# Three token mixers in another order: forgetting, then with sinks, then compressed

## The chip, the cores and the metric

The kernel runs on one core of a Trainium2 chip. Its engines are named as in the profile: PE (TensorE matmul), PEld (its weight loads), DVE (VectorE), ACT (ScalarE), POOL (GpSimd), SP (SyncE, which issues most DMAs). The metric is the device time of one execution in microseconds.

## What is computed

One layer of a decoder trunk on 1024 tokens of 1024 channels, in float32. One projection of the normalised input feeds three causal token mixers and the gates that merge them:

```
h = rms_norm(x, norm_mix);  cols = split_columns(h @ w_in)
o_a = nsa_mixer(...)   # A (number 0): compressed blocks, 8 selected blocks of 64 keys,
                       #   a window of 256, joined by sigmoid gates per head
o_b = swa_mixer(...)   # B (number 1): window of 128, with a learned sink per head
o_c = fox_mixer(...)   # C (number 2): dense causal, a cumulative log forget gate on the logits
branches = stack([o_a, o_b, o_c]);  proj = einsum('btnm,nmd->btnd', branches, w_branch)
gates = sigmoid(cols['merge']).reshape(b, t, 3, 1024)
x = x + (gates * proj).sum(axis=2) @ w_out
x = x + conv_ffn(rms_norm(x, norm_ffn), w_gate, w_up, conv_w, conv_b, w_down)
```

Each mixer has 8 heads of 64. The mixers don't need each other: any order of the three gives the same sum.

## The kernel before

Every product is made of three matmuls on halves that are rounded to a shorter format (high x high, high x low, low x high: lines 258 to 260). So each float32 operand is split first: ACT makes the high half (a CAST), DVE the low half (a subtraction). Weights are split in `wload` (raw `wraw`, halves `whi` and `wlo`, lines 234 and 235, two rows of 128 at a time).

The part that matters here is the woven one, from about 165 us on. The order on PE is written out there by a planner (class `Line`, `drive`), which merges three streams with its own clock and its own guesses of durations; the other engines are ordered by the scheduler around it.

- The first stream, `attend`, runs the mixers one after the other: `fox` (C), `mixer_a` (A), `mixer_b` (B). A unit of attention is two matmuls into an S bank (line 685, and 687 or 689), a minimum on DVE (704 or 700), an exp on ACT (713, `p<-S`), for B one more exp for the sink (753, `es`), sums and a reciprocal on DVE (754, 756), and a scaling of `p` on POOL (762). After each mixer its number is put as a mark into the queue of jobs.
- The second stream turns the scaled `p` (transposes into a T bank, line 797), splits the result on ACT and DVE (`pTh` 804, `pTl` 805) and multiplies it with V into the one O bank (820, 821). `out_bank` empties O (885 on ACT, 886 on DVE) and stores it to `s_o`.
- The third stream, `fill`, is dense work for the gaps: chunks of the projection by token (`tok_chunk`; 256 or 280 columns into a D bank, ACT copies at 426, squares and powers on POOL at 432 and 437, DVE at 435 and 440), then the 12 chunks of merge gates (`gate_chunks`; 512 columns, DVE 493, ACT 494), then the merges of two mixers. `merge(n)` waits for the mark of mixer n, loads its eight tiles of `s_o` into the `xl` buffers (line 1363), splits them (1364 on ACT, 1365 on DVE), and multiplies with `w_branch`.

The last gate chunk is made in another order (`lo_first`): it reads the low halves `xl` of the input first (line 512) so that `xl` comes free for the tiles of `s_o`, and then the high halves (484, 485). So the splits of the first merge fall beside the second half of this chunk.

There are 3 S banks, 2 T, 1 O and 2 D. What the streams leave of the fill when attention has ended is made densely; then `merge_last` does the third mixer and the rest of the program follows.

Of the kernel before, what the change touches and what calls it, by code (L numbers as in the profile page):

```python
# [167 lines left out]
class Builder:  # L168
# [291 lines left out]
    def gate_chunks(self, wp, sp, rbc):  # L460

        nc, a = self.nc, self.a
        for cc in (8, 9, 10, 11, 0, 1, 2, 3, 4, 5, 6, 7):
            n, r = divmod(cc * 256, D)
            w = self.wload(wp, a["w_in"], MERGE + cc * 256, 256, KD)
            for b in range(2):
                bs = slice(b * P, (b + 1) * P)
                for h in range(2):
                    hs = slice(h * 512, (h + 1) * 512)
                    if cc != 7 or b == 0:  # L470
                        yield self.d_free
                        p = self.dps()
                        yield from self.mm3_steps(p, [((w[k][0][:, bs], w[k][1][:, bs]),
                                                       (self.xh[k][:, hs], self.xl[k][:, hs])) for k in range(KD)],
                                                  b == 1 and h == 1)
                    else:
                        if h == 0:
                            ps = yield from self.lo_first(w, bs)
                        else:
                            yield lambda: 0.0  # L480
                        p = ps[h]
                        for k in range(KD):
                            yield lambda: 0.0
                            nc.tensor.matmul(p, w[k][0][:, bs], self.xh[k][:, hs], start=False, stop=False)
                            nc.tensor.matmul(p, w[k][1][:, bs], self.xh[k][:, hs], start=False, stop=(k == KD - 1))
                            self.line.pe(0.427)
                            if h == 1 and k % 2 == 1:
                                self.s_w.put(self.line.now)
                    t = self.line.on("V", self.line.now, 0.6)
                    self.s_d.put(t)  # L490
                    t = self.line.on("A", t, 0.52)
                    g = self.t(sp, [P, 512], F32, "stage", 3)
                    nc.vector.tensor_tensor(out=g, in0=p, in1=rbc[:, hs], op=ALU.mult)
                    nc.scalar.activation(g, g, AF.Tanh, scale=0.5)
                    out = self.s_gate[n, r + b * P:r + (b + 1) * P, hs]
                    if self.woven:
                        self.line.later(t + STORE, nc.sync.dma_start, out, g, tag="stage")
                    else:
                        nc.sync.dma_start(out, g)
# [1306 lines left out]
def run(gen):  # L1806
    for _ in gen:
        pass


def build(tc, a):
    with ExitStack() as ctx:
        b = Builder(tc, a)
        b.setup(ctx)
        pool = tc.tile_pool
        xp = b.xp = ctx.enter_context(pool(name="xp", bufs=1))
        wctx = ctx.enter_context(ExitStack())
        tp = wctx.enter_context(pool(name="tp", bufs=1))
        b.zero = b.t(tp, [P, 1], F32, "zero")
        tc.nc.vector.memset(b.zero, 0.0)  # L1820
        b.kc2 = b.t(tp, [P, P], F32, "kc2", 1)
        b.vc = [[b.t(tp, [P, P], F32R, f"vc{g}{j}", 1) for j in range(2)] for g in range(2)]
        wp = wctx.enter_context(pool(name="wp1", bufs=1))
        macc = [None] * KD
        b.mh, b.ml = {}, {}
        dense = ["D", "S", "S", "D", "S", "T", "T"]
        with pool(name="sp1", bufs=1) as sp:
            rbc = b.t(sp, [P, T], F32, "rbc", 1)
            tcm = b.t(sp, [P, NH, 128], F32, "tcm", 1)
            b.dcyc = ["D", "S", "S", "D", "S"]  # L1830
            with pool(name="s0", bufs=1) as s0:
                b.first(xp, s0, wp, sp)
            with pool(name="ctp", bufs=1) as ctp, pool(name="s1", bufs=1) as s0, pool(name="wpc", bufs=1) as wpc:
                wps = [wp, wpc]
                b.small = (wpc,)
                b.bias_rows(s0)
                b.cmp_table(tcm, s0)
                wins = [b.windows(ctp, which) for which in range(2)]
                run(b.tok_chunk(wps, sp, "cv1"))
                b.forget(s0)  # L1840
                b.compress(ctp, wps, 0, *wins[0])
                run(b.tok_chunk(wps, sp, "cq0"))
                b.compress(ctp, wps, 1, *wins[1])
                run(b.tok_chunk(wps, sp, "cv0"))
                for h in range(2):
                    b.bcast_cols(s0, b.rstd[:, h * 4:(h + 1) * 4], rbc[:, h * 512:(h + 1) * 512])
            with pool(name="ap1", bufs=1) as ap_, tc.manual_schedule(engines={mybir.EngineType.PE}):
                b.woven = True

                def attend():  # L1850
                    for n, mixer in ((2, b.fox(ap_)), (0, b.mixer_a(ap_, tcm)), (1, b.mixer_b(ap_))):
                        yield from mixer
                        b.jobs.append({"mark": n})
                    b.s_over = True

                def fill():
                    for n in ("ck1", "cq1", "ksvs", "kwvw", "aq0", "aq1", "bkv", "bq0", "bq1"):
                        yield from b.tok_chunk([wp], sp, n)
                    yield from b.gate_chunks([wp], sp, rbc)
                    for n in (2, 0):  # L1860
                        yield lambda: 0.0 if n in b.marks else NEVER
                        yield from b.merge(n, n == 2, macc, None, [wp], sp)

                b.dcyc = dense
                b.line.drive(attend(), b.t_stream(ap_), fill())
        b.dcyc = dense
        wctx.close()
        with pool(name="rp", bufs=1) as rp, pool(name="wq", bufs=1) as wq:
            b.wq = wq
            with pool(name="sp3", bufs=1) as sp:  # L1870
                b.out_proj(macc, b.merge_last(1, macc, rp, wq, sp), rp, wq, sp)
                last = b.gate_up(sp)
                with tc.manual_schedule(engines={mybir.EngineType.SP}):
                    b.down(last, rp)
# [50 lines left out]
```

## Time and profile before

| | us |
|---|---|
| median of three runs | 1880.89 (1880.38 to 1882.27) |
| the profiled execution | 1881.61 |
| its span, first to last instruction | 1879.8 |
| PE busy | 1842.3 (98%) |
| DVE busy | 1349.6 (72%) |
| ACT busy | 926.3 (49%) |
| POOL busy | 406.7 (22%) |

By the page's chain of the work that ended last, 90% of the span lies on PE. In time the woven part goes: C until about 460 us, A until about 917 us, B from 940 to 1046 us. Under C run the chunks by token; they end at about 523 us, in A. The gate chunks run from 515 to 978 us. The merge of C begins with its loads at 953 us, that of A at 1054 us; from 1064 us on `merge_last` makes that of B. An idle stretch of PE is read from the windows as length less busy time.

### The profile page before, as it was taken

What the parts mean: (1) busy time and instruction counts of PE and PEld (TensorE: products, weight loads), DVE (VectorE), ACT (ScalarE), POOL (GpSimd) and SP (SyncE); (2) the same over time, 40 slices, a digit from 0 to 9 for tenths busy, and PEclk for the clock granted to TensorE, in tenths of its full rate; (3) what the DMA queues carried; (4) which work ended last, traced back from release to release, by engine and by line L of the source; (5) the groups of instructions that cost most, each with busy time, mean ns of one, the idle gap of its engine ahead of it and who ended that gap; (6) DMA issues with size and microseconds to landing.
All of it is one profiled execution on the core that took longest, in us unless ns stands there. A gap on an engine that the chain in (4) does not pass through costs nothing.

```text
span 1879.8 us, 30674 instructions
## 1 busy us (share of the span) xinstructions
PE 1842.3 (98%) x10663; PEld 1619.8 (86%) x10663; DVE 1349.6 (72%) x2825; ACT 926.3 (49%) x1987; POOL 406.7 (22%) x586
## 2 busy tenths in 40 slices
PE   8999999999999999999989999999999999999999
PEld 8999999999988888888878888888888888878887
DVE  7664767776875666757688766669887778786865
ACT  4443566565544555546587523435443334344443
POOL 2223655565521423213232230000000000000000
PEclk9999999999999999999999999999999999999999
DMA  6345322233221132121343755534534434367433
GB/s 210 108 147 133 86 79 75 78 88 90 72 79 54 51 89 79 57 65 57 110 143 105 219 160 179 158 111 157 165 126 144 159 123 135 131 241 238 138 99 124
DMA packets 201471, 228.38 MB, mean 121 GB/s; under 512 B 43633, under 2 KB 149121, under 8 KB 201316
## 3 DMA queue, kind: packets, MB, share of 16 engines
q1 hardware_dynamic: 201252, 226.29, 39.0%
q8 instruction: 84, 1.38, 0.3%
q14 instruction: 71, 0.58, 0.1%
q0 software_dynamic: 64, 0.13, 0.0%
HBM read 162.12 MB, written 64.25 MB: 120 GB/s over the span
## 4 chain that ended last, share of the span: by engine, by line
PE 90%; DVE 5%; DMA 2%; ACT 2%; issue 1%; POOL 1%; SPq 0%; DVEq 0%; ACTq 0%; POOLq 0%
PE D L259 9%; PE D L258 9%; PE D L260 9%; PE T L797 5%; PE S L1574 3%; PE S L1572 3%; PE S L1573 3%; PE O L821 3%; PE O L820 2%; PE S L685 2%; PE T L1574 2%; PE T L1573 2%; PE T L1572 2%; PE D L1572 2%; PE D L1574 2%; PE D L1573 2%
## 5 line engine op out<-in xcount | busy, mean ns | idle before, releaser
L713 ACT ACTIVATE p<-S,mf 128x512 f32<-128x512 f32 (+3 forms) x320 | 174.4, 549 | 103.5 <-DVE mf L704 95.1
L805 DVE TENSOR_TENSOR pTl<-T,pTh 128x512 fp32r<-128x512 f32 (+2 forms) x248 | 150.9, 616 | 80.5 <-ACT pTh L804 78.8
L258 PE MATMUL D<-whi,xh 128*128 128x256 f32 (+2 forms) x680 | 199.0, 293 | 1.9 <-ACT whi L234 1.8
L1544 ACT CAST qhi<-qS 128x512 fp32r<-128x512 f32 x157 | 97.2, 622 | 205.4 <-PE O L1789 54.8
L259 PE MATMUL D<-wlo,xh 128*128 128x256 f32 (+2 forms) x680 | 192.6, 283 | 2.3 <-DVE wlo L235 2.3
L260 PE MATMUL D<-whi,xl 128*128 128x256 f32 (+2 forms) x680 | 192.1, 282 | 0.0
L804 ACT CAST pTh<-T 128x512 fp32r<-128x512 f32 (+2 forms) x248 | 128.3, 532 | 119.6 <-PE T L797 108.0
L259 PE MATMUL D<-xl,whi 128*128 128x512 f32 x448 | 176.6, 394 | 0.0
L762 POOL TENSOR_SCALAR p<-p,den,gates 128x384 f32<-128x384 f32 (+3 forms) x160 | 108.9, 694 | 270.5 <-DVE den L756 168.5
L258 PE MATMUL D<-xh,whi 128*128 128x512 f32 x368 | 152.2, 414 | 0.0
L1545 DVE TENSOR_TENSOR qlo<-qS,qhi 128x512 fp32r<-128x512 f32 x157 | 106.7, 687 | 56.0 <-ACT qhi L1544 55.2
L260 PE MATMUL D<-xh,wlo 128*128 128x512 f32 x368 | 145.0, 394 | 0.0
L797 PE MATMUL T<-c,p 128*128 128x128 f32 x864 | 129.7, 273 | 7.0 <-POOL p L762 4.1
L258 PEld LDWEIGHTS D<-whi,xh 128*128 128x128 f32 x680 | 128.6, 189 | 4.0 <-ACT whi L234 2.5
L259 PEld LDWEIGHTS D<-wlo,xh 128*128 128x128 f32 x680 | 128.8, 189 | 3.8 <-DVE wlo L235 2.9
L260 PEld LDWEIGHTS D<-whi,xl 128*128 128x128 f32 x680 | 128.6, 189 | 0.0
L235 DVE TENSOR_TENSOR wlo<-wraw,whi 128x512 fp32r<-128x512 f32 (+2 forms) x136 | 102.2, 760 | 31.5 <-ACT whi L234 25.5
L820 PE MATMUL O<-pTh,VV 128*128 128x256 f32 x448 | 119.4, 290 | 2.0 <-DVE osum L886 1.9
L821 PE MATMUL O<-pTl,VV 128*128 128x256 f32 x448 | 116.6, 284 | 2.4 <-DVE pTl L805 2.4
L762 POOL TENSOR_SCALAR p<-p,den 128x256 f32<-128x256 f32 (+3 forms) x160 | 90.5, 582 | 125.7 <-DVE den L756 47.9
L685 PE MATMUL S<-U,X 128*128 128x256 f32 (+2 forms) x320 | 107.8, 341 | 4.5 <-ACT p L713 4.3
L797 PEld LDWEIGHTS T<-c,p 128*128 128x128 f32 x864 | 100.9, 140 | 12.7 <-POOL p L762 7.9
(443 smaller groups left out, 5244.9 us busy)
## 6 DMA issues: line engine op xcount, KB each, us to landing
wraw<-w_in SPq DMA_DIRECT2D x96, 256.0 KB
s_gate<-stage SPq DMA_DIRECT2D x48, 256.0 KB
qraw<-w_up SPq DMA_DIRECT2D x24, 512.0 KB
qraw<-w_gate SPq DMA_DIRECT2D x22, 512.0 KB
xh<-w_down SPq DMA_DIRECT2D x22, 512.0 KB
s_sums<-xh SPq DMA_DIRECT2D x44, 256.0 KB
qS<-s_sums SPq DMA_DIRECT2D x44, 256.0 KB
s_act<-gc SPq DMA_DIRECT2D x20, 512.0 KB
```

Source lines behind the costliest of these rows:

```text
L258: nc.tensor.matmul(out, lh, rh, start=(k == 0), stop=False)
L259: nc.tensor.matmul(out, lh, rl, start=False, stop=False)
L260: nc.tensor.matmul(out, ll, rh, start=False, stop=(k == n - 1))
L685: nc.tensor.matmul(p, z["x"][:, z["qs"]], u[:, ks], start=True, stop=False)
L713: nc.scalar.activation(pt, z["tiles"][n][:, :w], AF.Exp, bias=z["m"], scale=-1.0, accum_out=den[:, n, q:q + 1])
L762: nc.gpsimd.tensor_scalar(pt, pt, d0[:, q:q + 1], 1.0 if gate is None else gate, op0=ALU.mult, op1=ALU.mult)
L797: nc.tensor.transpose(p[:, c0:c0 + P], z["t"][:, k:k + P], self.ident)
L805: nc.vector.tensor_tensor(out=pl[:, lo:hi], in0=p[:, lo:hi], in1=ph[:, lo:hi].bitcast(F32), op=ALU.subtract)
L820: nc.tensor.matmul(ow, vv[:, kj, :], parts["h"][:, cs], start=(b_first and s == 0), stop=False)
L821: nc.tensor.matmul(ow, vv[:, kj, :], parts["l"][:, cs], start=False, stop=(b_last and s == len(bank) - 1))
L1572: nc.tensor.matmul(p, lh[:, kk, :], rh, start=(first and kk == 0), stop=False, skip_group_check=True)
L1573: nc.tensor.matmul(p, lh[:, kk, :], rl, start=False, stop=False, skip_group_check=True)
```

## The change

The mixers run in the order C, B, A. The chunks by token follow: those of B before those of A. The gate chunks of B are made ahead of those of A, so that the chunk split in two halves is the last of A's (3 instead of 7). The two merges in the woven part are C's and B's, and `merge_last` takes A's.

```diff
-        for cc in (8, 9, 10, 11, 0, 1, 2, 3, 4, 5, 6, 7):
+        for cc in (8, 9, 10, 11, 4, 5, 6, 7, 0, 1, 2, 3):
...
-                    if cc != 7 or b == 0:
+                    if cc != 3 or b == 0:
...
-                    for n, mixer in ((2, b.fox(ap_)), (0, b.mixer_a(ap_, tcm)), (1, b.mixer_b(ap_))):
+                    for n, mixer in ((2, b.fox(ap_)), (1, b.mixer_b(ap_)), (0, b.mixer_a(ap_, tcm))):
...
-                    for n in ("ck1", "cq1", "ksvs", "kwvw", "aq0", "aq1", "bkv", "bq0", "bq1"):
+                    for n in ("ck1", "cq1", "bkv", "bq0", "bq1", "ksvs", "kwvw", "aq0", "aq1"):
...
-                    for n in (2, 0):
+                    for n in (2, 1):
...
-                b.out_proj(macc, b.merge_last(1, macc, rp, wq, sp), rp, wq, sp)
+                b.out_proj(macc, b.merge_last(0, macc, rp, wq, sp), rp, wq, sp)
```

What this does to the order is seen best at the crossing from the gates to the first merge. First ACT, before, where the eight splits of `s_o` tiles (L1364) begin; `p` with a 256-column S bank and `es` are B's:

```order
L804 CAST pTh_12364<-T_12359 128x512
L1364 CAST xl_2788_12726<-xl_2788_12726 128x512
L885 COPY osum_12383<-O_12332 64x512
L713 ACTIVATE p_12377,den_12355<-S_12373,mf_12354 128x256
L753 ACTIVATE es_12396<-mf_12354,sinks_71 128x1
L1364 CAST xl_2789_12730<-xl_2789_12730 128x512
L1364 CAST xl_2790_12734<-xl_2790_12734 128x512
L640 ACTIVATE X_12408<-T_12403,gain_65 64x512
L1364 CAST xl_2791_12738<-xl_2791_12738 128x512
L713 ACTIVATE p_12394,den_12355<-S_12390,mf_12354 128x256
L753 ACTIVATE es_12396<-mf_12354,sinks_71 128x1
```

The same place of ACT after; `p` of 384 columns is the window branch of A:

```order
L713 ACTIVATE p_12628,den_12618<-S_12622,mf_12617 128x384
L1364 CAST xl_2860_12957<-xl_2860_12957 128x512
L1364 CAST xl_2861_12961<-xl_2861_12961 128x512
L713 ACTIVATE p_12657,den_12618<-S_12651,mf_12617 128x384
L1364 CAST xl_2862_12965<-xl_2862_12965 128x512
L804 CAST pTh_12687<-T_12684 128x256
L713 ACTIVATE p_12674,den_12663<-S_12668,mf_12662 128x384
L1364 CAST xl_2863_12969<-xl_2863_12969 128x512
L1364 CAST xl_2864_12973<-xl_2864_12973 128x512
```

The splits stand among A's exps instead of B's, and the exps of sinks are gone from between them. On PE, before, the second half of the split gate chunk (L484, L485) is laid between B's logits (L685 and L687, 256 columns):

```order
L484 MATMUL D_12322<-xh_41_122,whi_12117 128x512
L485 MATMUL D_12322<-xh_41_122,wlo_12118 128x512
L685 MATMUL S_12475<-U_11944,X_12254 128x256
L687 MATMUL S_12475<-V_11945,X_12254 128x256
L484 MATMUL D_12322<-xh_42_123,whi_12123 128x512
L485 MATMUL D_12322<-xh_42_123,wlo_12124 128x512
L484 MATMUL D_12322<-xh_43_124,whi_12123 128x512
L485 MATMUL D_12322<-xh_43_124,wlo_12124 128x512
```

The same place of PE after, in A, whose logits of selected blocks (L689) are 384 and 512 columns wide:

```order
L484 MATMUL D_12602<-xh_42_123,whi_12440 128x512
L485 MATMUL D_12602<-xh_42_123,wlo_12441 128x512
L685 MATMUL S_12760<-U_11037,X_12019 128x384
L689 MATMUL S_12760<-V_11038,Y_12022 128x384
L685 MATMUL S_12770<-U_11037,X_12024 128x512
L689 MATMUL S_12770<-V_11038,Y_12027 128x512
L820 MATMUL O_12451<-pTh_12731,VV_11241 128x256
L821 MATMUL O_12451<-pTl_12732,VV_11241 128x256
```

The chunk's second half has moved from B to A. B itself stands after the change on PE beside chunks by token (L258 to L260 with 256 columns) at its start:

```order
L632 MATMUL T_6725<-c_6_69,qt_6450 128x128 x4
L685 MATMUL S_6741<-U_6161,X_6444 128x256
L687 MATMUL S_6741<-V_6162,X_6444 128x256
L820 MATMUL O_6747<-pTh_6613,VV_6254 128x256
L821 MATMUL O_6747<-pTl_6614,VV_6254 128x256
```

and a little further on, past two more logits, the fill beside it:

```order
L258 MATMUL D_6724<-whi_6702,xh_38_119 128x256
L259 MATMUL D_6724<-wlo_6703,xh_38_119 128x256
L260 MATMUL D_6724<-whi_6702,xl_46_127 128x256
L258 MATMUL D_6724<-whi_6702,xh_39_120 128x256
L259 MATMUL D_6724<-wlo_6703,xh_39_120 128x256
```

Before, the fill beside B was the end of the gate chunks and merge C.

## Rows read from the trace of the kernel before

**Rows 1.** Busy time in stretches: start:end, length, then each engine, clock, DMA.

```profile
core 0: us, PE busy (x) PEld busy (x) DVE busy (x) ACT busy (x) POOL busy (x), PEclk, DMA share, GB/s
165.00:262.00 97.00, 91.15 (x727) 89.13 (x726) 67.88 (x162) 56.08 (x136) 53.85 (x80) 0.98 0.39 104
262.00:460.00 198.00, 193.83 (x1560) 189.62 (x1559) 142.08 (x341) 120.89 (x292) 113.44 (x189) 1.00 0.31 85
460.00:940.00 480.00, 475.81 (x2870) 420.78 (x2869) 325.42 (x900) 259.15 (x628) 143.92 (x204) 1.00 0.25 72
940.00:1000.00 60.00, 52.89 (x319) 45.09 (x318) 51.48 (x159) 48.86 (x154) 17.81 (x36) 1.00 0.43 125
1000.00:1110.00 110.00, 108.83 (x570) 91.80 (x569) 81.23 (x180) 57.91 (x155) 37.26 (x46) 1.00 0.58 180
```

**Rows 2.** Waits of PE, total, times, longest: 262 to 460, 460 to 940.

```profile
PE D L258 <- ACT whi L234: 1.4, 1, 1.4
PE O L820 <- DVE osum L886: 1.3, 1, 1.3
...
PE T L797 <- POOL p L762: 1.7, 1, 1.7
```

**Rows 3.** PE in order of time: start, length, line, tiles; 512 and 256 columns.

```profile
600.12 0.40 PE L259 MATMUL D<-xl,whi 128*128 128x512 f32 x1
600.36 0.39 PE L260 MATMUL D<-xh,wlo 128*128 128x512 f32 x1
...
437.14 0.28 PE L259 MATMUL D<-wlo,xh 128*128 128x256 f32 x1
437.25 0.28 PE L260 MATMUL D<-whi,xl 128*128 128x256 f32 x1
```

**Rows 4.** Busy time in stretches: all of B, and two parts of it.

```profile
940.00:1046.00 106.00, 98.11 (x602) 85.16 (x601) 92.55 (x284) 86.23 (x272) 31.21 (x64) 1.00 0.41 120
955.00:985.00 30.00, 24.06 (x151) 20.28 (x150) 27.95 (x82) 28.04 (x85) 9.01 (x17) 1.00 0.59 176
985.00:1046.00 61.00, 60.22 (x374) 53.16 (x373) 54.19 (x165) 47.95 (x151) 18.19 (x38) 1.00 0.36 103
```

**Rows 5.** Groups by line in 940 to 1046 us: busy, mean ns, idle before.

```profile
L1387 DVE SCALAR_TENSOR_TENSOR xh<-stage,D 128x512 f32<-128x512 f32 x12 | 8.1, 678 | 1.1 <-PE D L260 1.1
L235 DVE TENSOR_TENSOR wlo<-wraw,whi 128x512 fp32r<-128x512 f32 x10 | 6.9, 695 | 0.7 <-ACT whi L234 0.7
L1365 DVE TENSOR_TENSOR xl<-xl 128x512 fp32r<-128x512 f32 x8 | 5.3, 685 | 0.7 <-ACT xl L1364 0.6
L493 DVE TENSOR_TENSOR stage<-D,rbc 128x512 f32<-128x512 f32 x4 | 2.7, 684 | 1.4 <-PE D L260 1.4
...
L753 ACT ACTIVATE es<-mf,sinks 128x1 f32<-128x1 f32 x64 | 18.5, 289 | 0.0
L234 ACT CAST whi<-wraw 128x512 fp32r<-128x512 f32 x10 | 6.0, 621 | 0.0
L1364 ACT CAST xl<-xl 128x512 fp32r<-128x512 f32 x8 | 4.7, 614 | 1.2 <-DMA xl<-s_o 1.2
L494 ACT ACTIVATE stage<-stage 128x512 f32<-128x512 f32 x4 | 2.5, 631 | 2.9 <-DVE stage L493 2.9
```

**Rows 6.** In order of time: ACT at the crossing, and a wait of PE.

```profile
955.57 0.62 ACT L1364 CAST xl<-xl 128x512 fp32r<-128x512 f32 x1 [1.23 <-DMA xl<-s_o]
...
968.40 0.39 PE L685 MATMUL S<-U,X 128*128 128x256 f32 x1 [1.40 <-ACT p L713]
```

**Rows 7.** Groups by line in 262 to 460 us, under chunks by token.

```profile
L426 ACT ACTIVATE stage<-D,rstd 128x256 f32<-128x256 f32 x38 | 16.4, 476 | 10.1 <-PE D L260 8.7 <-POOL Y L648 1.0
L235 DVE TENSOR_TENSOR wlo<-wraw,whi 128x512 fp32r<-128x512 f32 x16 | 13.7, 870 | 1.9 <-ACT whi L234 1.9
L440 DVE TENSOR_TENSOR stage<-stage,rr 128x256 f32<-128x256 f32 x18 | 7.9, 482 | 3.3 <-POOL rr L437 3.3
L435 DVE TENSOR_REDUCE rr<-sqh 128x8 f32<-128x512 f32 x10 | 6.7, 672 | 2.5 <-POOL sqh L432 2.5
```

## The prediction

> **What bounds the kernel now.** I first cut the part that the change can reach, 165 to 1110 us, into stretches [rows 1]. The reader is to see that TensorE is busy nearly throughout and that its idle time sits in places: 5.85 us of 97 before 262 us, 4.17 of 198 to 460, 4.19 of 480 to 940, 7.11 of 60 from 940 to 1000, 1.17 of 110 after. That is 22.5 us in all. After 1110 us the program is dense matmul work that the edit doesn't touch. So TensorE is the bound, its work is the same in both kernels (same matmuls, same shapes), and only these bubbles can change: the forecast is about where the new order opens and closes waits. Who ends the waits says that they are of several kinds [rows 2]: weights not yet split, the one O bank not yet emptied, a probability tile not yet scaled on POOL, an S bank not yet read by ACT.
>
> The busy figure hides some of the loss. A 512-column matmul is shown as 0.39 to 0.40 us long but the next one starts 0.23 us later; a 256-column one shows 0.28 and the next starts 0.11 to 0.12 later [rows 3]. So each wait costs about 0.16 us more than the idle time shown. The Trainium skill (Perfetto Trace Analysis, Identifying the Most-Contended Engine) says the same: matmul busy time is no good measure, since matmuls are pipelined. By its view a gain of eight removed waits would be 8 x 0.16 = 1.3 us larger than my sum of idle times; I leave that out of the sum.
>
> The worst place is 955 to 985 us: TensorE does 24.06 us of work in 30, while DVE and ACT are busy 27.95 and 28.04 [rows 4]. Two things meet there. The mixer with sinks (B) is heavy on ACT and DVE for little matmul work: every 256-column exp is followed by a 0.29 us exp of the sink [rows 5]. And the fill crosses from the gates to the merge of the forgetting mixer, which puts eight splits of s_o tiles on ACT (0.61 us each) and on DVE (0.69 us each), of which the first waits 1.23 us at the head of ACT for its DMA, with an osum copy and exps behind it in the order [rows 5, 6]. TensorE then stands for S banks, 1.40 us at 968.4 [rows 6]. Right after, from 985 to 1046, the same mixer under merge matmuls loses only 0.78 us of 61, with DVE at 54.19 and ACT at 47.95 [rows 4]. So it is the crossing inside B that costs, not B.
>
> **The change part by part.** *Up to the fourth token chunk* (about 273 us) TensorE's rows are the same in both programs: the third chunk is bkv for ksvs, of the same shapes. The 5.85 us before 262 us stay. 0.
>
> *The rest of the forgetting mixer (262 to 460 us, 4.17 us idle).* The chunks under it are bkv, bq0, bq1 and then ksvs, kwvw, instead of the A chunks first. The chunks' work is equal in sum; what moves is how they fall against the mixer. The waits here are accidents of spacing: 1.4 us for weights, 1.3 for the O bank [rows 2]. Summing the starts of rows 3 along the order, the shortest time after which TensorE comes back to the O bank is 1.2 us before and 2.8 us after; to a weight buffer 3.8 and 4.5 us. Bounds: 2 us lost (new accidents half as large again as the old) to 4.2 us gained. I take half, -2.0.
>
> *B earlier, under tokens and gates.* From B's first logits to its last, the order before holds 210 fill matmuls of 512 columns (0.23 each: 48 us) beside B's own 42 us; after, 297 of 256 columns (0.118) and 135 of 512, 66 us, beside 44. So B is spread over 110 us of matmul work instead of 90. Its own demand: in 940 to 1046 us DVE is busy 92.55 and ACT 86.23 [rows 4]; less the merge, gate, split and weight rows there (8.1 + 6.9 + 5.3 + 2.7 on DVE, 6.0 + 4.7 + 2.5 on ACT) [rows 5] that leaves 69.5 and 73.0. The fill under it after is 6.2 token banks, 5.6 gate blocks and the weight pairs of both: a token bank is two ACT copies of 0.476 us and 0.672 + 2 x 0.482 on DVE, a weight pair 0.62 on ACT and up to 0.87 on DVE [rows 7], a gate block 0.63 and 0.68 [rows 5]. Sum: 17 us on ACT, 23 on DVE. So ACT 90 and DVE 93 of 110: 82 and 84%. The nearest row is 985 to 1046 (ACT 79, DVE 89%, 0.78 lost in 61): 110 x 0.78 / 60.2 = 1.4 us lost. The upper bound is the rate of 955 to 985, if the token chunks' POOL work holds B's probabilities back; the lower is 0.
>
> *The crossing, now under A.* The eight splits stay, and fall between A's units. From the first to the last matmul of the split gate chunk the order holds 23.3 us of TensorE work after, 19.5 before. A's demand by 460 to 940 us [rows 1] is 325.42 / 475.81 = 0.68 us of DVE and 0.54 of ACT for one of TensorE: 15.9 and 12.7 us here, with the splits 21.4 and 17.6, or 92 and 76%. Before, DVE and ACT did 28 us against 24 of TensorE. So ACT, which held the S banks, gets room, and DVE is just under the matmuls. Bounds 0 and 5.9 us (the crossing as it was); I take 1.5, nearer to the row of 985 to 1046.
>
> Both together: B and its crossing lost 106 - 98.11 = 7.89 us [rows 4]; after 1.4 + 1.5. -5.0.
>
> *A itself.* The same units under the same gates; its end falls under merge matmuls instead of its beginning under tokens. Its largest wait, 1.7 us for POOL [rows 2], comes where TensorE transposes probabilities 1.7 us after their logits; after the edit the shortest such distance under A is 4.5 us. Against that, four transposed tiles near the crossing are used 1.3 to 2.1 us after they were made. I take -1.0 of the 4.19, with bounds -2 and +2.
>
> *What goes along unseen.* The near table of the mixer that follows is reloaded between B and A instead of between A and B; before, TensorE goes on with gates there (4.19 us idle in 480, the reload within) [rows 1], and gates are left at that point after too, so 0; without gates it would cost the landing time. The merges (2, then 1; the last one 0) find their marks long set, as now. The dense tail has the same shapes; 0.
>
> Sum: -2.0 - 5.0 - 1.0 = -8.0 us. The profiled execution took 1881.61 us (1879.8 of span and 1.8 around it), 0.7 above the median of 1880.89. 1881.6 - 8.0 = 1873.6, or 1872.9 on the median; I say 1873.
>
> **The rivals.** *No change: the crossing costs what it did.* The splits wait at the head of ACT wherever they stand [rows 6], DVE is at 92% by my sum, and new accidents under the forgetting mixer replace the old. Then the 5.9 us stay: 1.4 + 5.9 for B's 7.89, and 0 elsewhere: 1880.9 - 0.6 = 1880. For it: A brings a second selection (a chain of small DVE work) just ahead of the crossing. Against it: ACT at 76% instead of full. The Trainium skill speaks for this rival (TensorE: Matmul & The Clock Gate, Architectural detail): ACT and DVE queues are strictly first in, first out, so a waiting split blocks what is behind it in any mixer. The 1.23 us wait agrees [rows 6].
>
> *Slower: B under tokens saturates.* The token chunks bring POOL squares and powers, and DVE's weight splits take 0.87 us there against 0.695 in 940 to 1046 [rows 5, 7]. If B's first 60 us ran as 955 to 985 does (5.94 lost in 30), that is 12 us lost; with the crossing at 1.5 and the other terms at 0, against the 7.89 of now: 12 + 1.5 - 7.9 = 5.6 us more, 1886.5. It decides from the point where ACT or DVE of those 60 us comes above some 93% busy, as in rows 4.
>
> *More gain.* All idle time from 262 us but a third goes: 16.6 x 2/3 = 11 us, and 12 waits of 0.16: 1880.9 - 13 = 1868.
>
> That the planner doesn't do what the edit says is out: the order, with the starts of rows 3 summed along it, has B's logits at 434 to 554 us, and the crossing inside A.
>
> **How the numbers follow.** Forecast (1869 to 1877): 0.52. More gain (under 1869): 0.15. No change (1877 to 1884.6): 0.23. Slower: 0.10. About 0.2%, 3.8 us, is what a measurement of this kernel can tell from no change, so faster is under 1877.1: 0.67; same 0.23; slower 0.10. The range reaches into the neighbours on both sides: 1866 to 1882.
>
> **What would show it.** Right: the 30 us around the splits lose 1 to 3 us instead of 5.94, with ACT under 85%; B's 110 us lose under 2.5; no S-bank wait over 1 us in B. Wrong: B's stretch with ACT or DVE over 93% and TensorE idle above 5 us (slower), or waits for transposed tiles at the crossing of the old size (no change). Any change before 270 us or after the merges would be something I have not seen.

## The result, and the profile after

The changed kernel took 1891.84 us (median of four, 1890.38 to 1893.76) against 1880.98 for the kernel before in the same runs: ratio 1.0053, interval 1.0041 to 1.0064. It is slower by some 10 us; the prediction was 1873, faster by 8. The profiled execution took 1892.78 us (span 1891.0), 11.2 more than that of before. Before 165 us and after the woven part the two traces agree within 0.6 us.

The windows of the changed kernel over the same part, which answer to [rows 1] and [rows 4] (start:end, length, busy time and count of each engine, granted clock, DMA):

```profile
165.00:262.00 97.00, 91.31 (x716) 89.46 (x716) 67.43 (x158) 55.33 (x135) 52.67 (x79) 0.96 0.38 102
262.00:460.00 198.00, 197.33 (x1593) 193.62 (x1593) 144.99 (x359) 124.26 (x311) 114.97 (x190) 1.00 0.31 85
460.00:560.00 100.00, 94.15 (x669) 87.92 (x668) 82.53 (x247) 76.29 (x231) 46.56 (x68) 0.97 0.36 101
560.00:840.00 280.00, 278.89 (x1606) 242.39 (x1605) 184.63 (x504) 153.23 (x374) 75.34 (x121) 1.00 0.27 76
840.00:880.00 40.00, 35.78 (x195) 30.75 (x194) 23.93 (x72) 16.48 (x43) 9.01 (x14) 0.91 0.20 59
880.00:930.00 50.00, 50.00 (x304) 44.42 (x304) 32.03 (x104) 27.33 (x69) 15.46 (x25) 1.00 0.19 54
...
930.00:948.80 18.80, 15.77 (x86) 13.10 (x85) 15.54 (x37) 9.21 (x17) 0.00 (x0) 0.91 0.30 92
950.00:995.00 45.00, 40.73 (x229) 34.25 (x228) 35.62 (x105) 30.59 (x78) 15.70 (x19) 1.00 0.36 115
...
1000.00:1122.00 122.00, 121.03 (x621) 101.55 (x621) 77.20 (x154) 47.70 (x103) 36.44 (x36) 1.00 0.49 155
```

Two things are to be read. First, PE's idle time (length less busy time) over the whole part is 25.8 us against 22.5 before, only 3.3 more. Second, PE's *busy* time grew: 931.2 us for 6042 matmuls in 957 us after, 922.5 for 6038 in 945 before (a matmul on a border stands in two windows). The clock column says why: 0.96, 0.97, 0.91 where [rows 1] has 0.98 and 1.00. The forecast had no term for it.

The waits of PE over the whole run (engine, matmul and line, releaser: us in total, times, longest):

```profile
PE S L685 <- ACT p L713: 4.6, 5, 1.8
PE D L259 <- DVE wlo L235: 3.7, 2, 2.1
PE T L797 <- DVE pTl L805: 3.2, 1, 3.2
PE O L821 <- DVE pTl L805: 2.7, 5, 0.7
PE T L1179 <- DVE ce L1145: 2.4, 1, 2.4
PE T L797 <- POOL p L762: 2.4, 1, 2.4
PE T L1275 <- DVE mr L1168: 2.3, 1, 2.3
```

Single waits of 2 us and more have come in: 2.1 for a low half of a token weight at the start of B, 3.2 for a T bank at the end of B, 2.4 for `ce` (the compressed branch of A, line 1145, a chain of small DVE work), 2.3 for `mr` (A's selection of blocks, line 1168). Before, the only wait of this size in this part was that for POOL, 2.4 us just after 180 us; that one stands in both kernels. The windows around the four new ones, each cut where the granted clock (the TensorE clock that the profile shows as given to PE) fell:

```profile
470.00:477.80 7.80, 5.34 (x44) 4.95 (x42) 7.70 (x22) 6.45 (x20) 4.29 (x6) 1.00 0.67 200
477.80:481.20 3.40, 3.40 (x19) 3.40 (x18) 1.47 (x4) 0.00 (x0) 2.62 (x3) 0.50 0.35 99
548.00:556.30 8.30, 5.08 (x39) 4.69 (x38) 8.10 (x26) 8.16 (x27) 1.65 (x4) 1.00 0.54 153
556.30:559.70 3.40, 3.40 (x10) 2.64 (x9) 1.44 (x5) 1.14 (x4) 1.86 (x4) 0.50 0.32 96
853.00:856.70 3.70, 1.90 (x12) 1.54 (x10) 3.70 (x12) 2.04 (x7) 0.78 (x2) 1.00 0.75 198
856.70:863.50 6.80, 4.39 (x13) 3.31 (x14) 3.96 (x15) 2.49 (x7) 3.41 (x4) 0.50 0.28 83
939.00:945.40 6.40, 4.43 (x24) 3.55 (x24) 6.37 (x25) 1.38 (x3) 0.00 (x0) 1.00 0.56 174
945.40:948.80 3.40, 3.00 (x13) 2.62 (x14) 0.22 (x2) 1.96 (x4) 0.00 (x0) 0.50 0.05 17
```

In each pair the first row is at a clock of 1.00 (2.4 GHz) and the second at 0.50 (1.2 GHz). The first two waits end 0.7 and 1.1 us before the fall. The fall at 856.7 us came behind a wait of 1.8 us for an S bank (until 856.6 us), and the wait for `ce` lies in the row at 0.50, until 860.0 us. At 945.4 us the clock fell while PE still stood for `mr`, until 945.8 us. In all four first rows DVE is busy 98 to 100%, so what PE waited for stood among other VectorE work.

In all, the profile after has 23.9 us at 1.2 GHz between 165 us and the dense end, that of before 3.4. One of the stretches that came in, 3.41 us from 184.3 us on, stands behind the POOL wait that both kernels have, ahead of all that the change moves; it is not the change's. From the spacing of matmul starts against the median spacing of the same line and shape, a stretch of 3.41 us at 1.2 GHz loses some 1.5 us where matmuls follow each other. Summed over 165 to 1130 us, that is 9.1 us after and 1.5 before. All other excess over the median spacing, which is waiting, grew by some 2 us. So of the 9.7 us lost there by this count some 7.6 are matmuls at the lower clock and 2.1 are waits.

The profile of before (0.998) had a better clock than its other executions: over 49 of them the mean granted clock was 0.996, and over four of the changed kernel 0.993. By these means the clock is worth at most 0.003 x 1885 = 5.7 us of the 10.9 between the medians, an estimate; the profiles, with their 7.6, show more than its usual share.

### The profile page after: what moved, and what is told of

It is laid out like the page before. It is cut to its first block, busy times and chain, and to the rows that moved or that the text cites. A ratio compares the mean times of both kernels' runs of the same rounds, so it can differ in the third digit from the quotient of the medians.

```text
span 1891.0 us, 30662 instructions
## 1 busy us (share of the span) xinstructions
PE 1850.6 (98%) x10663; PEld 1626.1 (86%) x10663; DVE 1345.9 (71%) x2825; ACT 925.3 (49%) x1987; POOL 413.3 (22%) x586
## 4 chain that ended last, share of the span: by engine, by line
PE 91%; DVE 4%; DMA 1%; issue 1%; ACT 1%; POOL 1%; SPq 0%; ACTq 0%; DVEq 0%; POOLq 0%
PE D L259 10%; PE D L258 10%; PE D L260 10%; PE T L797 5%; PE O L821 3%; PE S L1573 3%; PE S L1574 3%; PE S L1572 3%; PE O L820 3%; PE S L685 3%; PE S L259 2%; PE S L260 2%; PE S L258 2%; PE T L1573 2%; PE T L1572 2%; PE T L1574 2%
## 5 line engine op out<-in xcount | busy, mean ns | idle before, releaser
L258 PE MATMUL D<-whi,xh 128*128 128x256 f32 (+2 forms) x680 | 200.2, 294 | 2.0 <-ACT whi L234 2.0
L260 PE MATMUL D<-whi,xl 128*128 128x256 f32 (+2 forms) x680 | 193.3, 284 | 0.0
L258 PE MATMUL D<-xh,whi 128*128 128x512 f32 x368 | 153.3, 417 | 0.0
L260 PE MATMUL D<-xh,wlo 128*128 128x512 f32 x368 | 146.2, 397 | 0.0
L258 PEld LDWEIGHTS D<-whi,xh 128*128 128x128 f32 x680 | 130.0, 191 | 4.0 <-ACT whi L234 2.6
L260 PEld LDWEIGHTS D<-whi,xl 128*128 128x128 f32 x680 | 129.9, 191 | 0.0
L235 DVE TENSOR_TENSOR wlo<-wraw,whi 128x512 fp32r<-128x512 f32 (+2 forms) x136 | 96.8, 723 | 29.2 <-ACT whi L234 28.8
L234 ACT CAST whi<-wraw 128x512 fp32r<-128x512 f32 (+2 forms) x136 | 83.0, 622 | 59.9 <-PE D L259 24.2
L685 PE MATMUL S<-U,X 128*128 128x256 f32 (+2 forms) x320 | 107.2, 341 | 4.6 <-ACT p L713 4.6
```

Of the source, the lines that this page charges most:

```text
L258: nc.tensor.matmul(out, lh, rh, start=(k == 0), stop=False)
L260: nc.tensor.matmul(out, ll, rh, start=False, stop=(k == n - 1))
L685: nc.tensor.matmul(p, z["x"][:, z["qs"]], u[:, ks], start=True, stop=False)
```

## The experiments

Ratios are to the kernel before on the same chip; us are differences worked out from them.

**The price of a wait by itself.** Four pauses were put into the dense merge of the kernel before, with 1, 2 or 3 ScalarE copies in each (the range of the loop; the line that sets `self.rbc` is left out here).

```diff
+    def pause(self):
+        z, o = self.rbc, self.ps("O")
+        nc.tensor.matmul(o[:, 0:32], z[:, 0:P], self.ident[:, 0:32], start=True, stop=True)
+        for _ in range(1):
+            nc.scalar.copy(z, z)
+        nc.tensor.matmul(o[:, 32:64], z[:, 0:P], self.ident[:, 0:32], start=True, stop=True)
...
+                    if not first and h == 1 and b == 0:
+                        self.pause()
```

> The kernel before, with four pauses of TensorE in the dense merge of mixer 0 after the woven part: after one bank of each of four groups, a matmul that reads rbc, one ScalarE copy of rbc in place (128x1024), and a matmul that reads the copy. The rest of TensorE's order stays. It measures the price of a wait by itself. From the durations of such copies (about 1.06 us) each pause is about 1.3 us. Theory 'waits and clock' (in the changed kernel, waits above 2 us cost more than themselves, since the granted clock falls to 1.2 GHz after them): short pauses cost themselves only, 4 x 1.3 = 5 us more than the kernel before, and no new stretch at 1.2 GHz. Theory 'waits only': the same, 5 us.

> As the run with four pauses of one copy, but two ScalarE copies in each: pauses of about 2.3 us, the size of three of the four longest waits of the changed kernel. Theory 'waits and clock': beside 4.2 us more of waiting than with one copy, some or all of the pauses are followed by a stretch at 1.2 GHz; up to 1.7 us each (half of the 3.41 us that such a stretch lasts in the trace of the changed kernel), so 6 to 11 us more than with one copy. Theory 'waits only': 4.2 us more, and the granted clock stays at 2.4 GHz or, where it falls, the time does not show it.

> As before, with three ScalarE copies in each of the four pauses: about 3.4 us each, the size of the longest wait of the changed kernel. Theory 'waits and clock': every pause is followed by a stretch at 1.2 GHz, so 8.4 us of waiting and 4 x 1.7 = 6.8 us of half clock more than with one copy, 15 us in sum. Theory 'waits only': 8.4 us more than with one copy.

Measured: 1890.37, 1896.56 and 1901.72 us; 1.0041 (1.0026 to 1.0056), 1.0074 (1.0059 to 1.0089) and 1.0100 (1.0085 to 1.0115), or 7.7, 13.9 and 18.8 us more than before. The fourth pause was filled by other matmuls, so three remain, and the expectations, made for four, are to be read at three quarters. Their waits with one, two and three copies, a line of each kernel:

```profile
PE O L1355 <- ACT rbc L1354: 5.9, 3, 3.5
```
```profile
PE O L1355 <- ACT rbc L1354: 8.9, 3, 4.4
```
```profile
PE O L1355 <- ACT rbc L1354: 12.0, 3, 5.3
```

The time beyond the waits is 1.8, 5.0 and 6.8 us. With three copies, the windows around the second and the third pause:

```profile
1088.00:1094.30 6.30, 2.96 (x16) 2.40 (x15) 0.69 (x1) 3.13 (x3) 1.79 (x2) 1.00 0.28 83
1094.30:1097.70 3.40, 3.40 (x10) 2.65 (x9) 1.08 (x2) 1.24 (x2) 0.00 (x0) 0.50 0.00 0
1104.00:1107.90 3.90, 2.00 (x11) 1.53 (x9) 0.69 (x1) 1.78 (x2) 2.40 (x2) 1.00 0.31 100
1107.90:1114.70 6.80, 5.36 (x14) 4.30 (x15) 0.00 (x0) 1.35 (x2) 0.08 (x1) 0.50 0.14 39
```

With one copy, the same second pause (a wait of 1.3 us) and the matmuls behind it:

```profile
1086.00:1089.00 3.00, 1.81 (x11) 1.48 (x10) 0.69 (x1) 1.04 (x1) 1.52 (x2) 1.00 0.64 186
1089.00:1092.00 3.00, 3.00 (x15) 2.42 (x14) 1.25 (x2) 1.24 (x2) 0.00 (x0) 1.00 0.30 87
```

After its pauses the trace has 3.4, 6.8 and 17.1 us at 1.2 GHz (one, two and three of the three pauses), and the spacing of starts inside them says 1.5, 3.0 and 6.6 us lost. That agrees with what is beyond the waits, within the intervals. From one copy to three the time grew by 11.1 us for 6.1 us of waiting; 'waits and clock' had 15 for four pauses, 'waits only' 8.4. With one copy 5 us and no fall were expected, and 7.7 came: the first pause, 3.5 us long since its copy began late, had a fall. The profile with three copies has another 6.8 us at 1.2 GHz ahead of the pauses, from 978 us on, which is not in these sums.

**One or two of the new waits taken out.** In A's code the planner places the transposes of the second group's selection 4 us later; in the second kernel also the transposes of one compressed chunk (the first line of the diff).

```diff
+                            e_t += 4.0 if (g, c) == (1, 0) else 0.0
...
-                            yield lambda: max(self.mr_t, self.s_t.peek())
+                            late = 4.0 if g == 1 else 0.0
+                            yield lambda: max(self.mr_t + late, self.s_t.peek())
```

> The changed kernel, with one wait taken out: in mixer 0 the planner places TensorE's transposes of the second group's selection 4 us later, so that other matmuls stand where it waited 2.30 us for the chain of small VectorE work (at 945.8 us), with a stretch at 1.2 GHz of 3.41 us right there. Theory 'waits and clock': the wait (2.3 us) and the stretch at 1.2 GHz (up to 1.7 us) both go: 2.3 to 4 us faster than the changed kernel, with one stretch at 1.2 GHz fewer. Theory 'waits only': 2.3 us. Theory 'queues full' (VectorE and ScalarE are the bound at the crossing): the wait comes back at the next tile that needs them, and the time stays within 1 us of the changed kernel.

> The changed kernel with two waits taken out by later places in TensorE's order: the transposes of the second group's selection (wait of 2.30 us at 945.8 us), and the transposes of the compressed branch's probabilities for one chunk (waits of 1.80 and 2.41 us at 856.6 and 860 us, with 6.83 us at 1.2 GHz around them). Theory 'waits and clock': 2.3 + 4.2 us of waits and up to 5.1 us of half clock go: 6 to 11 us faster than the changed kernel, 1881 to 1886. Theory 'waits only': 6.5 us faster at most. Theory 'queues full': the waits come back elsewhere, within 2 us of the changed kernel.

Measured: 1884.78 us (1.0015, 1.0005 to 1.0024) and 1878.98 (0.9983, 0.9974 to 0.9993). The first is 7 us faster than the changed kernel, the second 13, and 0.17% faster than the kernel before: just under what I count as a difference, though the interval leaves out 1. The windows where the waits stood, of the first kernel and then of the second:

```profile
943.00:948.00 5.00, 5.00 (x28) 4.07 (x27) 3.05 (x16) 0.46 (x1) 0.00 (x0) 1.00 0.32 113
...
930.00:1000.00 70.00, 65.97 (x370) 56.15 (x369) 54.20 (x150) 41.56 (x99) 17.80 (x24) 1.00 0.35 110
1000.00:1122.00 122.00, 122.00 (x630) 103.38 (x629) 81.78 (x160) 50.08 (x108) 36.95 (x36) 1.00 0.49 152
```
```profile
840.00:880.00 40.00, 38.17 (x229) 33.76 (x229) 26.60 (x88) 20.40 (x58) 11.32 (x18) 1.00 0.19 57
```

Both places are at clock 1.00 again. The idle time fell from 7.30 to 4.03 us (930 to 1000) with the first edit, which also took 0.97 us after 1000, and from 4.22 to 1.83 (840 to 880) with the second. Both gains exceed "waits only" (2.3 and 6.5 us) and also "waits and clock" (4 and 11): a wait taken out also moved the units behind it to better places. In the trace 4.2 us of the first gain are idle time from 930 us on, and some 1.5 us the stretch at 945 us; the stretch at 184 us is gone too, which the edit does not touch. B stands under the token chunks in both as it does in the changed kernel, and the second is still a little faster than the kernel before: so B under tokens doesn't decide the sign.

**Each part of the change alone.** The token chunks of the change in the kernel before; and the changed kernel with the old chunks.

```diff
-                    for n in ("ck1", "cq1", "ksvs", "kwvw", "aq0", "aq1", "bkv", "bq0", "bq1"):
+                    for n in ("ck1", "cq1", "bkv", "bq0", "bq1", "ksvs", "kwvw", "aq0", "aq1"):
```

> The kernel before with one part of the change alone: the new order of the token chunks (bkv, bq0, bq1 ahead of ksvs, kwvw, aq0, aq1). Mixers, gate chunks and merges stay as before. Theory 'waits and clock': the order of the chunks under the forgetting mixer is worth the 3.5 us of idle time that went there in the changed kernel (262 to 460 us), so 2 to 4 us faster than before as far as no new wait above 2 us comes where the mixer with sinks doesn't stand under tokens. Theory 'B under tokens' (the loss comes from the mixer with sinks under token chunks, which this kernel doesn't have): faster by 3.5 us too. If it is slower than before, the loss comes from the order of the chunks itself, and both theories miss it.

> The changed kernel with the token chunks in the order of before (ksvs, kwvw, aq0, aq1, bkv, bq0, bq1); mixers, gate chunks and merges in the new order. The mixer with sinks needs the last three chunks, so it can't start before all tokens are through, and stands wholly under gates. Theory 'waits and clock': the two waits of the start and the end of the mixer with sinks under token chunks (4.5 and 3.2 us, and their two stretches at 1.2 GHz) go, and the 3.5 us gained under the forgetting mixer go too; what is left is the wait in the compressed branch, in the selection and the crossing: 1883 to 1890. Theory 'B under tokens': all of the loss goes, 1877 to 1881. Theory 'mixers' (the order of the mixers costs by itself): 1890 or more.

Measured: 1904.92 us (1.0126, 1.0109 to 1.0143) and 1905.25 (1.0125, 1.0110 to 1.0140). For the chunks both theories missed, as the text allowed for a slower run; for the mixers two missed and 'mixers' (1890 or more) came. Each half costs 24 us where both together cost 10, so the halves don't add. They can't be read as prices of the two parts either, since each takes a mixer ahead of its own chunks: with the new chunks alone A comes second and its chunks last, with the new mixers alone B comes second and its chunks last. The logits (L685) alone, PE and PEld, in the kernel with the new chunks, in that with the new mixers and in the kernel before:

```profile
430.00:501.00 71.00, 0.21 (x1) 0.00 (x0) 1.00 0.35 102
```
```profile
435.00:510.00 75.00, 0.28 (x1) 0.00 (x0) 1.00 0.39 110
```
```profile
430.00:510.00 80.00, 7.69 (x25) 4.74 (x25) 1.00 0.30 81
```

For over 70 us PE makes fill without a logit, until the tokens are through, and the last product with V begins at 1091 and 1110 us instead of 1055 (before) and 1063 (whole change). The fill spent there is missing beside the mixers later; how much of the 24 us that makes, no run separates. From 600 us on PE waits, among others, for the same things as after the whole change, with the new chunks alone:

```profile
PE T L1275 <- DVE mr L1168: 5.3, 2, 3.0
...
PE T L1179 <- DVE ce L1145: 2.9, 1, 2.9
PE T L797 <- DVE pTl L805: 2.7, 1, 2.7
```

and from 480 us on with the new mixers alone:

```profile
PE T L797 <- DVE pTl L805: 3.2, 1, 3.2
PE T L1179 <- DVE ce L1145: 3.0, 1, 3.0
...
PE T L1275 <- DVE mr L1168: 2.0, 1, 2.0
```

Only the places in time differ (the wait for `ce` is at 759, 912 and, after the whole change, 860 us). They have 27.3 and 30.7 us at 1.2 GHz. The same chains exist in the kernel before (the product that makes `ce` takes 1.22 us in the median there and after the whole change), and its waits for `ce` and `mr` are zero: there PE found other work up to each. That the neighbours in the order make this difference is argued from it, and borne out by the two placements above.

**Longer guesses for the planner.** In the kernel before, every duration that the planner assumes on the other engines times 1.2; then in the best kernel so far (two waits out) only while B is planned (the diff), then there and at the crossing, then throughout.

```diff
+        dur *= 1.2 if 250 < self.now < 430 else 1.0
         t = max(ready, self.now) + self.HOP
```

> The kernel before with the planner's durations of every instruction 1.2 times as long (they are 15 to 30% below those of the trace), so that it puts other matmuls between a tile's making and its use. Nothing else changes. Theory 'waits and clock': waits and stretches at 1.2 GHz go in both orders; the kernel before has 16.6 us of idle time and few long waits from 262 us on, of which up to half goes: 1873 to 1881. If it is slower, the planner's short durations are not what leaves the waits.

> The kernel with two waits of mixer 0 taken out (the second group's selection and the compressed branch), and with the planner's durations of VectorE, ScalarE and GpSimd 1.2 times as long while it plans the mixer with sinks under the token chunks. The work and the order of the chunks stay; matmuls of the fill are only put more widely between the units. It asks whether the waits at the start (2.2 us, 1.2 GHz for 3.41 us) and at the end (3.4 us, the same) of the mixer with sinks are a matter of load or of spacing. Theory 'waits and clock' (spacing): both go, with half of 6.8 us at 1.2 GHz: 5 to 9 us faster than the kernel with two waits taken out, 1870 to 1874. Theory 'waits only': up to 5.6 us faster. Theory 'B under tokens' (VectorE and ScalarE are full there): the waits stay or move, within 2 us of 1879.

> As the run before this one, with the longer durations also while the planner plans the crossing from the gates to the merge (946 to 972 us of the trace, where TensorE waited 1.34, 1.15, 0.77 and 1.02 us). Theory 'waits and clock': some 3 of these 4.3 us go, with no stretch at 1.2 GHz to win there: 2 to 4 us faster than the run before this one. Theory 'queues full' (VectorE and ScalarE are the bound at the crossing): the time stays within 1 us.

> The kernel with two waits of mixer 0 taken out, with the longer durations all through the woven part. Theory 'spacing': every unit gets more matmuls between a tile's making and its use, so waits go in all mixers: 1866 to 1874. Against it: the same change to the kernel before made it 21 us slower, since the fill ran out under the last mixer. Here the last mixer ends some 100 us of the plan later too, so if the fill runs out again it is 1890 or more; then the fill that is spent early is what the last mixer lacks.

Measured: 1903.17 us (1.0111, 1.0096 to 1.0126), 1891.90 (1.0058, 1.0041 to 1.0075), 1886.03 (1.0023, 1.0011 to 1.0034) and 1911.69 (1.0161, 1.0146 to 1.0176). All four are slower than what they were made from, the first than the kernel before and the others than the kernel with two waits out. The forecasts of a gain over these missed, and for the last the warning (1890 or more) came true. In the kernel before with longer guesses:

```profile
PE T L259 <- DMA qS<-s_gate: 12.1, 1, 12.1
```
```profile
165.00:940.00 775.00, 766.82 (x5104) 701.27 (x5105) 520.85 (x1363) 424.76 (x1026) 299.95 (x455) 1.00 0.29 84
...
1090.00:1180.00 90.00, 70.73 (x333) 58.37 (x334) 63.53 (x132) 42.81 (x102) 8.52 (x17) 0.91 0.47 146
```

Up to 940 us it idles 8.2 us where the kernel before has 14.2 [rows 1], so the short guesses do leave waits. But the mixers end 59 us later (1114 for 1055 us), the fill is used up, and PE stands 12 us at the start of the last merge. The kernel with longer guesses throughout does the same (10.9 us there). With longer guesses under B alone:

```profile
452.00:594.00 142.00, 138.41 (x931) 125.73 (x930) 105.59 (x312) 98.13 (x296) 52.65 (x83) 1.00 0.34 95
...
930.00:1000.00 70.00, 61.15 (x340) 52.34 (x339) 50.00 (x129) 34.38 (x79) 12.04 (x19) 0.93 0.32 98
```

B's loss fell from 5.9 us (446 to 572 us in the kernel with two waits out) to 3.6, with the clock at 1.00. With more fill between its units DVE is also less busy under B, 74 instead of 79%, so this run doesn't part spacing from load. But 930 to 1000 us now loses 8.85 us at clock 0.93 (4.37 at 1.00 without), and 3.2 us are lost after it, which ate the gain: the selection's transposes (line 1278 there) had come into the crossing and waited 4.79 us. Planning the crossing wider too gave 6 us back, more than the 2 to 4 expected; 3.1 of them show in the profiles, where the selection waited 2.2 us. Two more kernels tell why: the first plans only the end of B wider, the second is the one with B planned wider, with the selection 12 us later.

```diff
-        dur *= 1.2 if 250 < self.now < 430 else 1.0
+        dur *= 1.2 if 370 < self.now < 430 else 1.0
```

```diff
-                            late = 4.0 if g == 1 else 0.0
+                            late = 12.0 if g == 1 else 0.0
```

> The kernel with two waits of mixer 0 taken out, with the planner's durations 1.2 times as long only at the end of the mixer with sinks, around the wait of 3.4 us at 551.6 us with its 3.41 us at 1.2 GHz. What follows is planned 4 us later, not 28 as with the whole mixer. Theory 'waits and clock': that wait and its stretch go, up to 5 us faster than the kernel with two waits taken out: 1874 to 1877, as far as 4 us more spacing don't bring the second selection and the crossing to a worse place. Theory 'the shift decides' (any shift of what follows draws the waits anew): 1880 or more.

> The kernel with longer durations through the whole mixer with sinks (1891.9), with the transposes of the second group's selection planned 12 us later in place of 4. In that kernel they stood at 964.6 us, inside the crossing, where TensorE waited 4.95 us for the selection and the clock was at 1.2 GHz for 10.2 us from 960.3 us on. Theory 'the shift decides' (the planner's new spacing moved the selection onto the crossing's splits): 5 us of waiting and up to 5 us of half clock go, 1882 to 1887. Theory 'the spacing itself costs' (the fill spent under the mixer with sinks is missing at the crossing): the wait moves to the next units, 1889 or more.

Measured: 1889.00 us (1.0038, 1.0024 to 1.0053) and 1887.04 (1.0025, 1.0015 to 1.0034). The second, in the crossing:

```profile
930.00:1000.00 70.00, 66.03 (x374) 56.19 (x373) 52.22 (x132) 36.38 (x83) 10.07 (x16) 1.00 0.38 117
```

One chain moved takes 4.9 us of idle time and the lower clock out of the place; 6 us of the 14 come back, though 2 us of new waits with 6.8 us at 1.2 GHz appear at 1042 us. So the place of one chain decided over these 6 us. For the other 8 the spent fill stays a rival: attention ends at 1084 us there, at 1055 in the kernel with two waits out. The first kernel speaks for the shift: it came out at 1889, what follows moved by only 4 us, the wait that it aimed at (3.2 us for `pTl`) stayed, and A's *first* group, covered until then, opened two:

```profile
PE T L1180 <- DVE ce L1146: 3.7, 1, 3.7
PE T L798 <- DVE pTl L806: 3.2, 1, 3.2
PE T L1278 <- DVE mr L1169: 2.3, 1, 2.3
```

## Why the prediction was wrong

Idle time of PE in us, from the windows:

| term | before | predicted change | after | change |
|---|---|---|---|---|
| up to the fourth chunk | 5.85 | 0 | 5.69 | -0.2 |
| rest of the forgetting mixer | 4.17 | -2.0 | 0.67 | -3.5 |
| B, with its crossing before and A's now | 7.89 | -5.0 | 5.85 + 4.27 | +2.2 |
| A without the crossing | 4.19 | -1.0 | 8.36 | +4.2 |
| the rest | 0.39 | 0 | 0.97 | +0.6 |
| sum of idle time | 22.49 | -8.0 | 25.81 | +3.3 |
| lost by matmuls at 1.2 GHz | 1.5 | no term | 9.1 | +7.6 |

The last two lines make 10.9 us of the 11.2 between the profiled executions. By the spacing of starts the waits grew by 2.1 us and not by 3.3; the two counts differ by that.

- *The forgetting mixer* was right in sign, and the gain larger than taken, within its bounds. That half of the idle time would go was a choice and not worked out.
- *B under tokens*: the loads came out near what I had worked out (82.5 of DVE and 76.3 of ACT in 100 us; I had 84 and 82%). The step from load to idle time failed: 1.4 us by the ratio of one steady row, against 5.85. In the 8 us around each of its two waits, up to the fall of the clock, DVE is busy 7.70 of 7.80 and 8.10 of 8.30 us. The rival "B under tokens saturates" had the right mechanism, but as two bursts of 8 us instead of 60 us, and it expected 93% over the stretch.
- *The crossing*: 4.27 us in 950 to 995 against 1.5 predicted and 5.94 before [rows 4]. ACT did fall to 68% there, as the step had it, and S-bank waits for ACT are still 2.6 us in sum. So the "no change" rival was nearly right on this term: the splits stand at the head of ACT under A too, three of them for 0.51, 2.81 and 0.72 us. The second of these, and PE behind it:

```profile
967.18 0.62 ACT L1364 CAST xl<-xl 128x512 fp32r<-128x512 f32 x1 [2.81 <-PE D L512]
...
968.42 0.50 PE L685 MATMUL S<-U,X 128*128 128x512 f32 x1 [1.28 <-ACT p L713]
```

But this rival gave the whole change 1880.
- *A itself* was the worst term of the idle time: 4.2 us lost, outside the bounds of -2 and +2. The POOL wait of 1.7 us went as forecast. But I looked at the distances of POOL's products and at transposed tiles, and did not follow A's two long chains of small DVE work, through `ce` to line 1179 and through `mr` to line 1275, to what covers them. In the trace of before they cost nothing, and so no row showed them. The taken-out waits show that these two, with what moved behind them, were worth 13 us of time.
- *The clock* was missing altogether. The prediction priced a wait at its length plus 0.16 us. The pauses show some 1.5 us on top for each 3.41 us at 1.2 GHz. It is the larger part of the loss in the profiles, also without the 1.5 us at 184 us that are not the change's.

No case of mine had the time that came: the slower rival was worked out as 1886.5, and all that is slower had a chance of 0.10.

What stays open: which place a chain lands in after a change of order. The runs show that 4 us of shift redraw the waits, not a way to foresee them short of following each chain against the measured durations.

## What to carry to other kernels

In a program whose bound engine is 98% busy and whose order was set by a planner, a change of order is not priced by average loads. List the long dependent chains of the moved parts, with durations from the trace, and ask for each what the bound engine does meanwhile in the new order. A chain that shows no wait before is covered by its neighbours, which the change can take away. Move the dense work that a part needs along with the part: without that, 71 to 75 us went by without a logit here. Then count long single waits apart from the sum of idle time, since each can have a stretch at the lower clock beside it, and look at the clock column of the windows beside the busy time; afterwards move the few long chains singly (two edits of 4 us brought 13 us here) instead of making every guess safer.

## What the hardware showed that I had not expected

That the granted clock falls is not told by a wait's length alone. After a wait of 2.36 us at 184.0 us it fell in the changed kernel; after one of 2.83 us at the same matmul it stayed in the kernel with two waits taken out. In the profile of the kernel before it stayed after 2.36 us there too, and its one fall in the woven part came at 231.0 us, behind a wait of 1.6 us. The changed kernel and the kernel with two waits out:

```profile
184.30:187.70 3.40, 3.40 (x17) 3.40 (x16) 2.99 (x5) 0.91 (x3) 2.50 (x4) 0.51 0.50 135
```
```profile
182.00:186.00 4.00, 4.00 (x32) 3.91 (x33) 3.94 (x7) 1.03 (x3) 2.76 (x4) 1.00 0.56 157
```

At 1.2 GHz there are 17 matmuls in 3.4 us, at 2.4 GHz 32 in 4.0. The clock varies between executions of one kernel too: the kernel with only the end of B planned wider took 1883.6 us at a mean clock of 0.996 and 1888.7 to 1891.7 at 0.993 to 0.994. So part of that kernel's spread goes with the clock. The Trainium skill (TensorE: Matmul & The Clock Gate, HAM oscillation) tells of a kernel whose TensorE falls back to half clock at every wait for data and pays for it each time; the rows at 0.50 beside waits here agree, at some 1.5 us for 3.4 us, but not every wait here has one.
